# Order of the products, queries by token, and adjoining decay products in a hybrid decoder block on one core

## The chip, the core and the metric

The kernel runs on one core of a Trainium2 chip. What is measured is the device time of one execution in microseconds, the median of several runs. A NeuronCore has TensorE (matmuls, which write to PSUM), VectorE, ScalarE and GpSimd (elementwise work), and queues that issue DMA transfers; each engine works through its own instructions in order and waits for the others by semaphores. In the profile, PE is TensorE's matmuls, PEld its weight loads, DVE VectorE, ACT ScalarE, POOL GpSimd and SP the engine that issues most transfers.

## The reference

One decoder layer on 256 tokens with a model width of 2048, all in float32:

```python
h = rms_norm(x, norm_mix_w)
q, k, v, z, xbc, dt_raw, gate_a, gate_s = split(h @ w_in)      # 16960 columns
q = rms_norm(q per head, q_norm_w); k = rms_norm(k per head, k_norm_w)
attn = sliding_window_attention(q, k, v, attn_sinks, rel_bias_table) @ w_attn_out   # 32 heads of 64, 4 kv heads
ssm = mamba2_mixer(z, xbc, dt_raw, ...) @ w_ssm_out            # 64 heads of 64, 8 groups, chunks of 128
x = x + (sigmoid(gate_a) * attn + sigmoid(gate_s) * ssm) @ w_out
u = causal_depthwise_conv(rms_norm(x, norm_ffn_w) @ w_ffn_up)
g, up = split(u); x = x + (gelu(g) * up) @ w_ffn_down          # 5632 wide
x = x + sigmoid(rms_norm(x, ple_norm_w) @ w_ple_gate) * (p @ w_ple_proj)
```

In the mixer, `seg = exp(a_cum[l] - a_cum[s])` below the diagonal is the decay between two tokens of a chunk, and `y_diag = (cb * seg) @ xdt` is the product with it, per head and chunk. In the attention, a token sees the 128 tokens up to itself, with a bias by distance and one extra "sink" logit per head.

## The kernel before

Activations lie transposed, features on the 128 partitions and the 256 tokens along the row. Precision beyond one pass comes from splitting: a value is stored as a high part (rounded to the matmul's type) and a low part (the rest). An activation tile such as `XS[:, k, :]` holds the high parts of 256 tokens and then the low parts, 512 columns. The weights come from memory in chunks of 512 KB (four blocks of 128 rows, 256 output columns). `load_chunk` (L68) starts the transfer, lets ScalarE write the high part `wh` (L77) and VectorE the low part `wl` (L78); there are three buffers of each. `products` (L81) is one block of weights against one activation block: the high weights against all 512 columns (L84) and the low weights against the first 256 (L83, L86). The sum of the PSUM tile's two halves, which `summed` makes (L109), is the result.

A `panel` (L92) makes 256 output columns, that is two feature tiles of 128, each in a PSUM tile of its own (`acc`, four buffers). For every chunk it runs the four k of the first tile and then the four k of the second. `by_token` (L482) does the same with the roles exchanged, tokens on the partitions of the result: three matmuls of 256 columns for each k and half of the tokens (L494 to L496). Only keys and values use it.

The stages follow one another: the state-space mixer in 8 groups of five panels (two of `xc`, one of B and C, two of `z`); eight panels of its gate; `w_ssm_out`; keys and values; attention; `w_attn_out`; `w_out`; 44 panels of the feed-forward's first weight and the second weight; the gated embedding. The instructions are written in this order, but a planner orders those of each engine by a simulated timeline, in which the earlier written goes first when it is ready. So in the trace a panel's long products sometimes run one ahead of the short ones.

In a group of the mixer, GpSimd makes the decay exponents of one chunk (`E`, L359 and L360, 1024 columns, one buffer), ScalarE their exponential (L361), VectorE multiplies by `cbm` (L362), TensorE makes eight heads' products, alternately in the upper and the lower half of the output's partitions (L366), and VectorE adds the skip term (L370). Then the same comes for the second chunk, whose `E` needs the first one's buffer.

In the attention 16 panels alternate by `ATT_ORDER`: three of queries, then gate and query in turn, then three of gates. A query panel ends as two transposed tiles `qc`, one for each pair of heads. After every chunk of a panel `advance` gives each running `attend` one turn; at most three run at once, and a new one may start in each turn. An `attend` goes through five turns: (1) its bias is fetched, `head_rstd` gets the heads' norms from squares with four statistics matmuls (L472) and a power on GpSimd (L477), and the queries are split into `Q`, high part in the own half of the partitions and low part in the other; (2) scores with high and low keys (L557, L558), the latter with 64 rows, then scale and bias on VectorE; (3) softmax; (4) transposes (L590); (5) the output products (L597 to L599).

## Time and profile before

| | |
|---|---|
| median of 3 timed runs | 2117.54 us (2113.01 to 2117.91) |
| profiled execution, its own time | 2113.4 us |
| its span, first to last instruction | 2111.6 us |
| mean granted TensorE clock | 0.995 of full speed |
| busy: PE, PEld, DVE, ACT, POOL | 2094.0, 1815.8, 1511.2, 1176.4, 182.6 us |
| matmuls, VectorE and ScalarE instructions | 12228, 2526, 1775 |
| read from memory | 381 MB, 182 GB/s over the span |

Busy time of PE is time with at least one matmul in flight; the matmuls overlap, so what one costs is read from the starts of its neighbours. A wait of an engine that does not set the end costs nothing. In the rows below, "xN" merges N neighbouring instructions of one kind into one line, whose start is that of the first.

### The profile page before, as it was taken

Reading aid. Unit: us, or ns where it says so; the run is one execution under the profiler, and the core shown is the slowest. Engines: PE = TensorE matmul, PEld = TensorE weight load, DVE = VectorE, ACT = ScalarE, POOL = GpSimd, SP = SyncE. Lnnn points to the kernel's source line nnn. Section 1 sums busy time; section 2 is a strip of 40 time slices with the busy share of each in tenths; the row PEclk is TensorE's granted clock in tenths of the full one; section 3 lists DMA queues with packets and bytes.
Section 4 is the critical chain, followed back from the end, with each engine's and each line's share of the span. In section 5 each row is a group of like instructions: output and inputs, shape, how many; then the busy total and the mean of one; then the engine's idle time right before and its main releaser. Section 6 shows DMA issues by size and latency. Waiting matters only on the chain.

```text
span 2111.6 us, 32047 instructions
## 1 busy us (share of the span) xinstructions
PE 2094.0 (99%) x12228; PEld 1815.8 (86%) x12228; DVE 1511.2 (72%) x2526; ACT 1176.4 (56%) x1775; POOL 182.6 (9%) x122
## 2 busy tenths in 40 slices
PE   7999999999999999999999999999999999999999
PEld 6888888888888888888888888888888888888888
DVE  7888888888655456767667777777777776455576
ACT  5766766666544434656464556555555555444454
POOL 3212122211000000000000020000000000000000
PEclk8999999999999999999999999999999999999999
DMA  5565555555555555444335655555555555555564
GB/s 192 207 201 176 192 180 190 187 192 170 180 190 189 183 187 198 145 154 163 126 125 194 228 188 188 187 189 190 186 184 188 190 187 186 186 189 186 175 208 145
DMA packets 113302, 385.47 MB, mean 183 GB/s; under 512 B 14075, under 2 KB 21116, under 8 KB 111996
## 3 DMA queue, kind: packets, MB, share of 16 engines
q1 hardware_dynamic: 104060, 366.00, 50.5%
q10 hardware_dynamic: 9088, 17.43, 2.4%
q8 instruction: 95, 1.56, 0.3%
q14 instruction: 59, 0.48, 0.1%
HBM read 381.17 MB, written 2.21 MB: 182 GB/s over the span
## 4 chain that ended last, share of the span: by engine, by line
PE 96%; issue 1%; DVE 1%; DMA 1%; ACT 0%; POOL 0%; SPq 0%; ACTq 0%; POOLq 0%
PE acc L84 59%; PE acc L86 28%; PE acc L83 2%; PE ms L558 1%; PE ms L557 1%; PE ms L366 1%; PE ms L590 1%; PE acc L90 1%; DVE wl L78 0%; PE ms L597 0%; PE ms L84 0%; PE ms L472 0%; PE ms L346 0%; PE ms L377 0%; PE ms L599 0%
## 5 line engine op out<-in xcount | busy, mean ns | idle before, releaser
L78 DVE TENSOR_TENSOR wl<-raw,wh 128x1024 fp32r<-128x1024 f32 (+1 forms) x700 | 862.8, 1233 | 477.3 <-ACT wh L77 470.1
L77 ACT ACTIVATE wh<-raw 128x1024 fp32r<-128x1024 f32 (+1 forms) x700 | 733.0, 1048 | 655.4 <-PE acc L84 476.0
L84 PE MATMUL acc<-XS,wh 128*128 128x512 f32 x2048 | 717.4, 400 | 7.0 <-ACT wh L77 7.0
L84 PE MATMUL acc<-XG,wh 128*128 128x512 f32 x1632 | 559.2, 395 | 0.0
L86 PE MATMUL acc<-XS,wl 128*128 128x256 f32 x1920 | 533.9, 286 | 4.6 <-DVE wl L78 4.6
L84 PEld LDWEIGHTS acc<-XS,wh 128*128 128x128 f32 x2048 | 375.6, 191 | 77.8 <-ACT wh L77 7.2
L86 PE MATMUL acc<-XG,wl 128*128 128x256 f32 x1530 | 412.6, 281 | 0.0
L86 PEld LDWEIGHTS acc<-XS,wl 128*128 128x128 f32 x1920 | 365.2, 190 | 24.1 <-DVE wl L78 9.6
L84 PEld LDWEIGHTS acc<-XG,wh 128*128 128x128 f32 x1632 | 293.2, 188 | 54.0
L86 PEld LDWEIGHTS acc<-XG,wl 128*128 128x128 f32 x1530 | 287.1, 188 | 14.1
L84 PE MATMUL acc<-FS,wh 128*128 128x512 f32 x704 | 245.5, 397 | 0.0
L86 PE MATMUL acc<-FS,wl 128*128 128x256 f32 x688 | 189.5, 281 | 0.0
L84 PE MATMUL acc<-YS,wh 128*128 128x512 f32 x512 | 178.2, 395 | 0.0
L84 PEld LDWEIGHTS acc<-FS,wh 128*128 128x128 f32 x704 | 129.6, 188 | 28.5
L86 PE MATMUL acc<-YS,wl 128*128 128x256 f32 x496 | 137.0, 282 | 0.0
L86 PEld LDWEIGHTS acc<-FS,wl 128*128 128x128 f32 x688 | 129.2, 188 | 3.0
L112 ACT ACTIVATE lo<-acc 128x256 f32<-128x256 f32 x158 | 59.7, 383 | 93.9 <-PE acc L84 93.9
L84 PEld LDWEIGHTS acc<-YS,wh 128*128 128x128 f32 x512 | 94.1, 188 | 20.2
L662 POOL TENSOR_TENSOR sqa<-sqa,rsq 128x256 f32<-128x256 f32 x30 | 32.6, 1088 | 883.7 <-ACT rsq L661 882.8
L86 PEld LDWEIGHTS acc<-YS,wl 128*128 128x128 f32 x496 | 93.1, 188 | 2.2
L84 PE MATMUL acc<-AS,wh 128*128 128x512 f32 x256 | 88.5, 397 | 0.2 <-DVE sum L114 0.2
L84 PE MATMUL acc<-MS,wh 128*128 128x512 f32 x256 | 87.7, 396 | 0.0
(250 smaller groups left out, 2222.1 us busy)
## 6 DMA issues: line engine op xcount, KB each, us to landing
raw<-in_w_in SPq DMA_DIRECT2D x260, 512.0 KB, 3.3
raw<-in_w_ffn_up SPq DMA_DIRECT2D x176, 512.0 KB, 3.2
raw<-in_w_ffn_down SPq DMA_DIRECT2D x88, 512.0 KB, 3.2
raw<-in_w_ssm_out SPq DMA_DIRECT2D x64, 512.0 KB, 3.2
raw<-in_w_attn_out SPq DMA_DIRECT2D x32, 512.0 KB, 3.2
raw<-in_w_out SPq DMA_DIRECT2D x32, 512.0 KB, 3.3
raw<-in_w_ple_gate SPq DMA_DIRECT2D x32, 512.0 KB, 3.2
acb<-acd ACTq DMA_DIRECT2D x8, 1024.0 KB, 6.3
```

Of the source, the lines that this page charges most:

```text
L77: S.activation(wh[:, ks, :], raw[:, ks, :], AF.Copy)
L78: V.tensor_tensor(wl[:, ks, :], raw[:, ks, :], wh[:, ks, :].bitcast(F32), ALU.subtract)
L83: TE.matmul(ps[:, 0:T], lhsT=wl, rhs=x[:, 0:T], start=False, stop=False, skip_group_check=True)
L84: TE.matmul(ps, lhsT=wh, rhs=x, start=first, stop=last)
L86: TE.matmul(ps[:, 0:T], lhsT=wl, rhs=x[:, 0:T], start=False, stop=False, skip_group_check=True)
L90: TE.matmul(ps[:, 0:T], lhsT=w, rhs=x[:, h * T:(h + 1) * T], start=first and n == 0, stop=last and n == 2)
L112: S.activation(lo, ps[:, T:2 * T], AF.Copy)
L366: TE.matmul(py[r * HD:(r + 1) * HD, j * P:(j + 1) * P], lhsT=xdt[:, c, h * HD:(h + 1) * HD], rhs=E[:, h, :], start=True, stop=True)
L557: TE.matmul(ss[h][:, cs], lhsT=Q[:, h, qs], rhs=kh[g][:, ks], start=True, stop=False)
L558: TE.matmul(ss[h][:, cs], lhsT=Q[half[h], h, qs], rhs=kl[g][half[h], ks], start=False, stop=True)
L590: TE.transpose(pt[:, d * P:(d + 1) * P], Ls[:, h, c:c + P], ident)
L662: G.tensor_tensor(sqa, sqa, sq, ALU.add)
```

## The change

`products` takes both feature tiles of a block: high weights of tile one and two, then low weights of tile one and two. `panel` goes over k with both tiles in step, and so do the last panel (`products_joined`) and the embedding. In the mixer `decays` makes both chunks' exponentials at the start of a group, with two buffers of `E` (and one of `zg` in place of two); the product with the state, `po`, comes before the decay products, which follow one another for both chunks in two PSUM tiles. In attention the queries are made by token; `normed` takes the norms along the row (a square on ScalarE, a reduction on VectorE, the power on GpSimd) and scales the queries; `attend` has a first turn that only fetches the bias, then transposes its two heads' queries. The low keys' product takes all 128 rows. The order of the output products alternates between the two heads. `ATT_ORDER` puts the eight query panels into the first eleven.

```diff
@@ -37,8 +37,7 @@
-ATT_ORDER = ([("q", 0), ("q", 1), ("q", 2)] + [x for n in range(5) for x in (("g", n), ("q", n + 3))]
-             + [("g", 5), ("g", 6), ("g", 7)])
+ATT_ORDER = [(x[0], int(x[1])) for x in "q0 q1 q2 g0 q3 q4 g1 q5 q6 g2 q7 g3 g4 g5 g6 g7".split()]
@@ -78,16 +77,20 @@
-    def products(ps, wh, wl, x, first, last):
-        if last:
...
+    def products(ps2, wh, wl, x, first, last):
+        tiles = [slice(i * P, (i + 1) * P) for i in range(2)]
+        for ps, cs in zip(ps2, tiles):
+            TE.matmul(ps, lhsT=wh[:, cs], rhs=x, start=first, stop=False, skip_group_check=True)
+        for ps, cs in zip(ps2, tiles):
+            TE.matmul(ps[:, 0:T], lhsT=wl[:, cs], rhs=x[:, 0:T], start=False, stop=last, skip_group_check=True)
@@ -97,12 +100,10 @@
                 wh, wl = load_chunk(src[base + j])
-            for ct in range(2):
-                cs = slice(ct * P, (ct + 1) * P)
...
+            for k in range(KC):
+                kk = j * KC + k
+                (products_joined if joined else products)(ps, wh[:, k, :], wl[:, k, :], xs[:, kk, :],
+                                                          kk == 0, kk == nk - 1)
             if between:
@@ -213,6 +214,18 @@
         nc.sync.dma_start(gno, a["ssm_norm"])
+        def decays(acb, hs):
+            Es = []
+            for c in range(2):
+                E = sp.tile([P, 8, P], F32, name="E", bufs=2)
+                sa = bc(acs[:, c, hs].unsqueeze(2), [P, 8, P])
+                G.tensor_tensor(E, acb[:, :, c, :], sa, ALU.subtract)
+                G.tensor_tensor(E, E, bc(tri.unsqueeze(1), [P, 8, P]), ALU.mult)
+                S.activation(E, E, AF.Exp)
+                Es.append(E)
+            return Es
@@ -307,6 +320,7 @@
                 acb = sums_of_group(g)
+                Es = decays(acb, hs)
             xc = sp.tile([P, 4, T], F32, name="xc")
@@ -317,6 +331,7 @@
                     acb = sums_of_group(0)
+                    Es = decays(acb, hs)
                 for i in range(2):
@@ -351,30 +366,28 @@
-            yg = sp.tile([P, 4, T], F32, name="yg", bufs=1)
-            for c in range(2):
...
...
                 TE.matmul(po[:, js], lhsT=xde[:, js], rhs=cbm[:, 1, :], start=True, stop=True)
+            yg = sp.tile([P, 4, T], F32, name="yg", bufs=1)
+            for c in range(2):
+                E = Es[c]
+                V.tensor_tensor(E, E, bc(cbm[:, 2 * c, :].unsqueeze(1), [P, 8, P]), ALU.mult)
+            pys = [misc(), misc()]
+            for c in range(2):
+                for h in range(8):
+                    j, r = h // 2, h % 2
+                    TE.matmul(pys[c][r * HD:(r + 1) * HD, j * P:(j + 1) * P],
+                              lhsT=xdt[:, c, h * HD:(h + 1) * HD], rhs=Es[c][:, h, :], start=True, stop=True)
+            for c in range(2):
+                cs = slice(c * P, (c + 1) * P)
+                for j in range(4):
+                    V.scalar_tensor_tensor(yg[:, j, cs], xc[:, j, cs], dsk[:, 4 * g + j:4 * g + j + 1],
+                                           pys[c][:, j * P:(j + 1) * P], ALU.mult, ALU.add)
             ec = sp.tile([P, 512], F32, name="ec", bufs=1)
@@ -456,31 +469,31 @@
         V.tensor_scalar(nsink, sink, -1.0, None, ALU.mult)
         gq = ap.tile([P, 2], F32, name="gq", bufs=1)
...
-        def head_rstd(t, scale, nm):
-            sq = ap.tile([P, T], F32, name="hsq")
-            S.activation(sq, t, AF.Square)
-            st = misc()
+        def normed(ps2):
+            qm = ap.tile([P, 2, 4], F32, name="qm")
             for b in range(2):
-                TE.matmul(st[:, 2 * b:2 * b + 2], lhsT=sq[:, b * P:(b + 1) * P], rhs=blk64, start=True, stop=True)
-            v = ap.tile([P, 2, 2], F32, name="hv")
+                sq = ap.tile([P, 256], F32, name="ksq")
+                S.activation(sq, ps2[b][:, 0:PW], AF.Square, scale=HD ** -0.5)
+                V.tensor_reduce(qm[:, b, :], sq.rearrange("p (h d) -> p h d", h=4), AX.X, ALU.add)
+                V.tensor_scalar(qm[:, b, :], qm[:, b, :], r2_tok[:, b:b + 1], EPS, ALU.mult, ALU.add)
+            p = ap.tile([P, 2, 4], F32, name="qp")
+            G.tensor_tensor(p, qm, bc(mhalf[:, 0:1].unsqueeze(2), [P, 2, 4]), ALU.pow)
+            r = ap.tile([P, 2, 4], F32, name="qr")
+            qn = ap.tile([P, 2, PW], F32, name="qn", bufs=3)
             for b in range(2):
-                V.tensor_scalar(v[:, b, :], st[:, 2 * b:2 * b + 2], r2_tok[:, b:b + 1], EPS, ALU.mult, ALU.add)
-            p = ap.tile([P, 2, 2], F32, name="hp")
...
+                V.tensor_scalar(r[:, b, :], p[:, b, :], r_tok[:, b:b + 1], HD ** -0.5, ALU.mult, ALU.mult)
+                V.tensor_tensor(qn[:, b, :].rearrange("p (h d) -> p h d", h=4),
+                                ps2[b][:, 0:PW].rearrange("p (h d) -> p h d", h=4),
+                                bc(r[:, b, :].unsqueeze(2), [P, 4, HD]), ALU.mult)
+            return qn
+        def by_token(between=None):
@@ -494,6 +507,8 @@
                         TE.matmul(ps2[b][:, 0:PW], lhsT=lo, rhs=wh[:, k, :], start=False, stop=(kk == ND - 1))
+                if between:
+                    between()
             base += CH
@@ -538,30 +553,32 @@
-        def attend(i, qc):
+        def attend(i, qn):
...
             bias = pair_bias(i)
-            rq = head_rstd(qc, HD ** -0.5, "rq")
+            yield
+            qt = misc()
+            cs = slice((i % 2) * P, (i % 2 + 1) * P)
+            for b in range(2):
+                TE.transpose(qt[:, b * P:(b + 1) * P], qn[:, b, cs], ident)
             Ls = ap.tile([P, 2, 384], F32, name="Ls", bufs=3)
...
             for h in range(2):
-                S.activation(Q[half[h], h, :], qc[half[h], :], AF.Copy)
-                V.tensor_tensor(Q[half[1 - h], h, :], qc[half[h], :], Q[half[h], h, :].bitcast(F32), ALU.subtract)
+                S.activation(Q[half[h], h, :], qt[half[h], 0:T], AF.Copy)
+                V.tensor_tensor(Q[half[1 - h], h, :], qt[half[h], 0:T], Q[half[h], h, :].bitcast(F32), ALU.subtract)
             yield
             ss = [misc(), misc()]
-            for cs, ks, qs in ((slice(0, 256), slice(0, T), slice(P, T)), (slice(256, 384), slice(P, T), slice(0, P))):
-                for h in range(2):
+            for h in range(2):
+                for cs, ks, qs in ((slice(0, 256), slice(0, T), slice(P, T)),
+                                   (slice(256, 384), slice(P, T), slice(0, P))):
                     TE.matmul(ss[h][:, cs], lhsT=Q[:, h, qs], rhs=kh[g][:, ks], start=True, stop=False)
-                    TE.matmul(ss[h][:, cs], lhsT=Q[half[h], h, qs], rhs=kl[g][half[h], ks], start=False, stop=True)
+                    TE.matmul(ss[h][:, cs], lhsT=Q[:, h, qs], rhs=kl[g][:, ks], start=False, stop=True)
             for h in range(2):
-                s = ss[h]
-                V.scalar_tensor_tensor(Ls[:, h, 0:256], s[:, 0:256], rq[:, 1, h:h + 1], bias[:, h, :],
...
+                V.tensor_tensor(Ls[:, h, 0:256], ss[h][:, 0:256], bias[:, h, :], ALU.add)
+                V.tensor_tensor(Ls[:, h, 256:384], ss[h][:, 256:384], bias[:, h, 0:P], ALU.add)
             nm = ap.tile([P, 2, 2], F32, name="nm")
@@ -591,12 +608,12 @@
             o = misc()
-            for h in range(2):
-                rows = slice(h * HD, (h + 1) * HD)
...
+            vs = slice(g * HD, (g + 1) * HD)
+            for cs, b, ks, f, e in ((slice(0, P), 0, slice(0, P), True, True),
+                                    (slice(P, T), 0, slice(P, T), True, False),
+                                    (slice(P, T), 1, slice(T, 384), False, True)):
+                for h in range(2):
+                    TE.matmul(o[h * HD:(h + 1) * HD, cs], lhsT=vt[:, b, vs], rhs=pts[:, h, ks], start=f, stop=e)
             split(AS[:, i, :], o[:, 0:T])
@@ -610,14 +627,15 @@
         for kind, pn in ATT_ORDER:
+            if kind == "q":
+                qn = normed(by_token(advance))
+                waiting += [(2 * pn, qn), (2 * pn + 1, qn)]
+                continue
             ps2 = panel(W, base, ND, XS, between=advance)
...
             for i in range(2):
-                if kind == "q":
-                    waiting.append((2 * pn + i, summed(ps2[i], "qc", 5, ap)))
...
+                t = summed(ps2[i])
+                V.tensor_tensor(GA[:, 2 * pn + i, :], t, r_bc, ALU.mult)
         while waiting or running:
```

## Rows read from the trace of the kernel before

**Rows 1.** The chain that ended last, by line: share of the span.
```profile
PE acc L84 59%; PE acc L86 28%; PE acc L83 2%; PE ms L558 1%; PE ms L557 1%; PE ms L366 1%; PE ms L590 1%; PE acc L90 1%; DVE wl L78 0%; PE ms L597 0%; PE ms L84 0%; PE ms L472 0%; PE ms L346 0%; PE ms L377 0%; PE ms L599 0%
```

**Rows 2.** Busy time by stage: window, its length, PE, PEld, DVE, ACT, POOL, clock, DMA.
```profile
50.00:520.00 470.00, 469.66 (x2878) 408.84 (x2877) 408.10 (x672) 308.99 (x404) 104.23 (x53) 1.00 0.56 189
...
797.00:1105.00 308.00, 307.55 (x1869) 259.81 (x1867) 210.59 (x492) 175.94 (x372) 19.56 (x17) 0.99 0.45 151
...
1262.00:1757.00 495.00, 495.00 (x2824) 432.07 (x2823) 382.10 (x701) 291.65 (x442) 3.98 (x3) 1.00 0.54 188
```

**Rows 3.** Waits over the span: who for whom, us in total, times, longest.
```profile
ACT wh L77 <- PE acc L84: 476.0, 288, 5.9
...
PEld acc L86 <- DVE wl L78: 9.6, 11, 2.5
```

**Rows 4.** Timeline of PE, first panel of the ssm output: start us, us.
```profile
616.84 0.28 PE L86 MATMUL acc<-YS,wl 128*128 128x256 f32 x1
616.96 0.39 PE L84 MATMUL acc<-YS,wh 128*128 128x512 f32 x1
...
617.89 0.28 PE L86 MATMUL acc<-YS,wl 128*128 128x256 f32 x1
618.01 0.39 PE L84 MATMUL acc<-YS,wh 128*128 128x512 f32 x1
...
619.40 0.63 PE L84 MATMUL acc<-YS,wh 128*128 128x512 f32 x2
619.86 0.28 PE L86 MATMUL acc<-YS,wl 128*128 128x256 f32 x1
...
620.91 0.40 PE L86 MATMUL acc<-YS,wl 128*128 128x256 f32 x2
621.15 0.40 PE L84 MATMUL acc<-YS,wh 128*128 128x512 f32 x1
```

**Rows 5.** Timeline of PE in the values by token, 14 matmuls from first to last.
```profile
815.01 0.28 PE L494 MATMUL acc<-wh,XS 128*128 128x256 f32 x1
...
816.60 0.28 PE L496 MATMUL acc<-wh,XS 128*128 128x256 f32 x1
```

**Rows 6.** Timeline of PE in attention: output products, statistics, scores, next panel.
```profile
1078.06 0.43 PE L597 MATMUL ms<-pts,vt 128*64 128x128 f32 x2
...
1078.83 0.38 PE L599 MATMUL ms<-pts,vt 128*64 128x128 f32 x2
1079.14 0.61 PE L472 MATMUL ms<-blk,hsq 128*128 128x2 f32 x4
1079.61 0.36 PE L557 MATMUL ms<-kh,Q 128*128 128x256 f32 x1
...
1081.86 0.50 PE L84 MATMUL acc<-AS,wh 128*128 128x512 f32 x1
```

**Rows 7.** Timeline of PE in attention: six transposes and what follows.
```profile
1073.96 0.88 PE L590 MATMUL ms<-c_ident,Ls 128*128 128x128 f32 x6
1074.59 0.36 PE L86 MATMUL acc<-AS,wl 128*128 128x256 f32 x1
```

**Rows 8.** Timeline of PE in the mixer: second chunk's decay products and their neighbours.
```profile
96.38 0.40 PE L86 MATMUL acc<-XS,wl 128*128 128x256 f32 x2
96.71 1.09 PE L366 MATMUL ms<-E,xdt 128*64 128x128 f32 x16
97.73 0.94 PE L377 MATMUL ms<-cbm,xde 128*128 128x128 f32 x6
```

**Rows 9.** Timeline of POOL in the mixer: decay exponents.
```profile
158.95 2.74 POOL L360 TENSOR_TENSOR E<-E,tri 128x1024 f32<-128x1024 f32 x1
```

**Rows 10.** Timeline of DVE in the same stretch.
```profile
159.52 3.25 DVE L394 TENSOR_TENSOR yg<-yg,zg 128x1024 f32<-128x1024 f32 x1
```

**Rows 11.** That line's instructions: ns min/median/max, first and last start.
```profile
L394 DVE TENSOR_TENSOR yg<-yg,zg x8: 1211/3244/3320, 100.4 to 532.0; 128x1024 f32<-128x1024 f32 x8
```

**Rows 12.** Groups of instructions: count, busy us, mean ns, idle before.
```profile
L86 PEld LDWEIGHTS acc<-XS,wl 128*128 128x128 f32 x1920 | 365.2, 190 | 24.1 <-DVE wl L78 9.6
```

More of the change, by code (lines that the diff above doesn't have):

```diff
@@ L79, in load_chunk, with products_joined @@
         return wh, wl
-    def products(ps, wh, wl, x, first, last):
-        if last:
-            TE.matmul(ps[:, 0:T], lhsT=wl, rhs=x[:, 0:T], start=False, stop=False, skip_group_check=True)
-        TE.matmul(ps, lhsT=wh, rhs=x, start=first, stop=last)
-        if not last:
-            TE.matmul(ps[:, 0:T], lhsT=wl, rhs=x[:, 0:T], start=False, stop=False, skip_group_check=True)
-    def products_joined(ps, wh, wl, x, first, last):
-        for n, (w, h) in enumerate(((wh, 0), (wh, 1), (wl, 0))):
-            TE.matmul(ps[:, 0:T], lhsT=w, rhs=x[:, h * T:(h + 1) * T], start=first and n == 0, stop=last and n == 2)
+    def products(ps2, wh, wl, x, first, last):
[4 more added lines that the diff above has]
+            TE.matmul(ps[:, 0:T], lhsT=wl[:, cs], rhs=x[:, 0:T], start=False, stop=last, skip_group_check=True)
+    def products_joined(ps2, wh, wl, x, first, last):
+        for i, ps in enumerate(ps2):
+            cs = slice(i * P, (i + 1) * P)
+            for n, (w, h) in enumerate(((wh, 0), (wh, 1), (wl, 0))):
+                TE.matmul(ps[:, 0:T], lhsT=w[:, cs], rhs=x[:, h * T:(h + 1) * T], start=first and n == 0,
+                          stop=last and n == 2)
     def panel(src, base, nk, xs, before=None, between=None, joined=False):
@@ L99, in panel @@
                 wh, wl = load_chunk(src[base + j])
-            for ct in range(2):
-                cs = slice(ct * P, (ct + 1) * P)
-                for k in range(KC):
-                    (products_joined if joined else products)(
-                        ps[ct], wh[:, k, cs], wl[:, k, cs], xs[:, j * KC + k, :],
-                        j * KC + k == 0, j * KC + k == nk - 1)
+            for k in range(KC):
+                kk = j * KC + k
+                (products_joined if joined else products)(ps, wh[:, k, :], wl[:, k, :], xs[:, kk, :],
+                                                          kk == 0, kk == nk - 1)
             if between:
@@ L383, in hybrid_block @@
             V.tensor_tensor(yg[:, :, P:T], yg[:, :, P:T], ec.rearrange("p (j l) -> p j l", j=4), ALU.add)
-            zg = sp.tile([P, 4, T], F32, name="zg", bufs=2)
+            zg = sp.tile([P, 4, T], F32, name="zg", bufs=1)
             for pn in range(2):
@@ L708, in embedding @@
             wh, wl = load_chunk(a["w_ple_proj"][pn], 2, PW)
-            es = []
-            for i in range(2):
-                cs = slice(i * P, (i + 1) * P)
-                ps = misc()
-                for k in range(2):
-                    products(ps, wh[:, k, cs], wl[:, k, cs], PS_[:, k, :], k == 0, k == 1)
-                es.append(summed(ps, "ple", 4, pp))
-            return es
+            ps2 = [misc(), misc()]
+            for k in range(2):
+                products(ps2, wh[:, k, :], wl[:, k, :], PS_[:, k, :], k == 0, k == 1)
+            return [summed(ps, "ple", 4, pp) for ps in ps2]
         for pn in range(8):
```

34 lines of the change are left out of this document (removed).

## The prediction

> **What bounds the kernel now.** I read the chain of waits by line first, then the engines' busy time stage by stage, and only then single instructions. The chain that ended last runs through TensorE: 59% of the span through the long product of `products` (L84, the weight's high part against 512 columns) and 28% through the short one (L86, the low part against 256) [rows 1]. TensorE has work in flight without a break in the stages of [rows 2]. So a change counts by what it does to TensorE's starts, unless it makes an engine that feeds TensorE late. Three stages matter: the state-space stage (50 to 520 us), where VectorE is busy in 408 of 470 us; attention (797 to 1105 us), 211 of 308 us; and the plain panels, for which 1262 to 1757 us stands [rows 2]. Almost nothing is lost there to data that is late: TensorE's weight loads waited 9.6 us in all for a low part, whereas ScalarE waited 476 us for TensorE to give a buffer back [rows 3]. What a matmul costs is the time from its start to the next start, since the durations overlap; every price below is such a difference.
>
> The sum is made against the profiled execution's own 2113.4 us (span 2111.6 and 1.8 around it). The median of the three timed runs is 2117.5, their lowest 2113.0, so the profile lies at the fast end of them.
>
> **Part 1, the order inside `products`.** Before, a panel runs four k of one feature tile, long, short, long, short, and then four of the other. After, each k runs long, long, short, short, every one into the other PSUM tile than the one before it. It is 2592 such steps of four matmuls: 161 panels of 16 k (40 state-space, 8 gates, 16 for the ssm output, 8 gates in attention, 8 and 8 for the two output weights, 44 up, 22 down, 7 for the last gate) and 16 in the embedding. No matmul and no weight load is added or removed. All four kinds of step between neighbours stand in the trace of before, though rarely, because the planner already lets one run ahead. Long and short in turn: from 616.96 to 619.40 us seven pairs take 2.44 us, 0.349 each. Long after long: 0.46 us for two, 0.23 each, what a long one takes before a short one (0.349 less 0.12). Short after short: 0.24 for two, 0.12 each, as 616.84 to 616.96. And the change of tile at 618.01, where by the code the fifth pair begins in the other bank, comes 0.12 after its forerunner, like a step within one bank [rows 4]. So the four cost 0.70 us in either order, and I take 0 for this part. Its ends are wide because 2592 steps multiply anything: the by-token product of keys and values, which has the roles of weight and activation swapped, does 14 matmuls of 256 columns in 1.59 us, so 768 columns in 0.341 against 0.349 [rows 5]. If alternation reached that, it would be 5184 pairs by 0.009, 46 us less. At the other end, the timeline is resolved to 0.01 us; that much on two of the four steps is 52 us more.
>
> **Part 2, queries by token.** (a) A query panel becomes 96 matmuls of 256 columns, 96 by 0.1136 = 10.9 us [rows 5], for 32 pairs at 0.349 = 11.2 us: 0.26 us by 8 panels = 2.1 us less.
> (b) The score products, eight per pair of heads: the half-height ones against `kl` (64 rows) become full height. Before, the eight take from 1079.61 to 1081.86 us, 2.25 us [rows 6]; there are 16 pairs. Plain matmuls of 256 columns take 0.114 to 0.12, and those of 128 columns 0.105 by the transposes (six in 0.63 us) [rows 7]: four and four make 0.89 to 0.90. That is 1.35 by 16 = 21.6 us less, the largest term. If half of the present cost is not due to the height, 11 us; nothing excludes that, but ordinary matmuls of these widths stand in the same stage at the lower price.
> (c) The four statistics matmuls of a pair go (1079.14 to 1079.61, 0.47 us [rows 6]); two transposes come, 0.21 us by the same six [rows 7]: 0.26 by 16 = 4.2 us less.
> (d) The output products, twelve recorded matmuls in 1.08 us (1078.06 to 1079.14 [rows 6]), get the alternation of column halves that the decay products have, 16 in 1.02 us [rows 8], 0.064 each: 0.77, so 0.31 by 16 = 5.0 us less; 0 if the planner had already reached what alternation gives.
> (e) On the other engines a pair loses a square, four small VectorE operations, one GpSimd power and the sum into `qc`; a panel gains two squares, two reductions, four small operations, two products and one power. VectorE's work per pair stays about even, so I cost it at nothing: TensorE covers it, with 308 us to VectorE's 211 [rows 2]. In the new order q panels crowd into the first eleven, and an `attend` has six turns and an end where it had five and an end; three at a time give 12/7 = 1.7 pairs per panel, all through by the 13th panel. If the cover is thin there, the splits of the next weight chunk are late; I allow 3 us.
>
> **Part 3, the state-space stage.** The two chunks' decay products adjoin. Each stands now as a run of its own: the two short matmuls before it take 0.33 us to its start instead of 0.24 [rows 8], so an entry costs 0.09; the exit lies between 0 and 0.18, as the last two output products of a pair take 0.31 us to the next kind (1078.83 to 1079.14 [rows 6]) where two within a run take 0.13. One entry and exit less in each of 8 groups: 0.7 to 2.2, I take 1.5 us less. The 4 GpSimd operations of a group move to its start, past the conv of the first panels; the exponentials go with them, ahead of ScalarE's weight copies. No DMA is added on a queue, and the bias and sums transfers are issued in the same order. The cover is the group's three panels of 11.2 us before the decays are multiplied. GpSimd's time collides with VectorE though: at 158.95 GpSimd begins 2.74 us on the decays, and VectorE's product of `yg` and `zg`, started at 159.52, takes 3.25 us; the same line's shortest is 1.21 [rows 9 to 11]. I allow 4 us for where the moved ones fall. The two-tile burst on VectorE (two products of this shape, 1.2 us each) also lies in that allowance.
>
> The Trainium skill, SBUF — State Buffer, "Who interferes with whom", says that a VectorE instruction with two SBUF inputs and a GpSimd instruction that reads SBUF exclude each other for a whole instruction. The trace agrees with 3.25 against 1.21 us. That rule speaks against this change, as the weight split itself has two SBUF inputs; its result is the third rival.
>
> **The end.** Both tiles of the last panel now finish together, so their last vector operations queue: below 1 us, taken as 0.3.
>
> **Sum.** 2113.4 - 2.1 - 21.6 - 4.2 - 5.0 - 1.5 + 3 + 4 + 0.3 = 2086.3; as the timed median lies a little above the profile, I say 2088 us.
>
> **Rivals.**
> 1. Alternation speeds the stream. For: the by-token products show that 768 columns can pass in 0.341 us [rows 5]. Against: those stay in one bank, and the present change of bank saves nothing [rows 4]. 2088 - 46 = 2042 us.
> 2. VectorE becomes the bound while queries crowd. VectorE's 211 us in attention less 72 splits (18 panels of four) at the 1.21 us that this shape takes undisturbed [rows 11] leave 124, 7.7 per pair with all around it. At 1.7 pairs a panel that is 4.9 + 13.1 = 18.0 us, against TensorE's 10.9 + 1.7 by some 2.5 = 15.2. Over 9 panels 25 us late, in place of the 3 allowed: 2110 us. Against: the durations overlap by several hundredths each, which makes 18.0 too high, and whatever is late can run in the last five g panels.
> 3. GpSimd blocks the weight splits. The second chunk's two operations (at most 2.74 us each [rows 9]) now lie in one run with the first's; if each holds up a split for its whole length and none of it is absorbed, 5.5 by 8 = 44 us in place of 4: 2128 us, no gain left. Against: VectorE has 62 us idle in that stage [rows 2], and as many such operations ran before. Half of it is likelier, 2106.
> 4. Slower: two short matmuls in a row leave no long one under which the next weight load hides. A load shows 0.19 us, so the short one's 0.12 already leans on overlap [rows 12]. It decides from 25/2592 = 0.010 us a step; at 0.02 a step it is 52 us, 2140 us. Against: short after short at 0.12 in the trace, but only now and then, never twice a step.
> That the planner does not follow the written order is possible too; it then undoes part 1, which is 0, and changes nothing here.
>
> **How the numbers follow.** Forecast 0.58, rival 1 0.14, rival 2 0.10, rival 3 0.08, rival 4 0.10. The forecast's own range is 2072 to 2102. From 2040 to 2118 leaves out rival 4, and the ends of 1 and 3, together 0.2. A measurement of this kernel can tell 0.3% from no change, 6 us: faster is below 2111. Faster: the forecast, rival 1, and most of rivals 2 and 3 (0.11 of 0.18), 0.83; within 0.3%: the rest of these two but for 0.01, and 0.02 of rival 4, 0.08; slower: the other 0.09.
>
> **What would show it.** Right: in the plain stages the step of four stays at 0.70 us, and 1262 to 1757 us still needs 495; attention shrinks by some 30 us; the eight score products take 0.9 us; no new wait of the weight loads for L78's line. Wrong: steps of 0.68 or 0.72 in the plain panels (rivals 1 and 4); VectorE near full between the first and eleventh panel of attention with TensorE waiting for low parts (2); weight splits of 3 us beside GpSimd at a group's start (3).

## The result and the profile after

The changed kernel takes 2090.05 us (median of four runs, 2089.55 to 2093.43), the kernel before beside it 2115.28: a ratio of 0.9884, 95% interval 0.9865 to 0.9904. Forecast were 2088 us. The profiled execution after took 2089.55 us (span 2087.7), 23.85 less than the 2113.4 of before. The total is right; by stages it is not made of the terms of my sum.

Where a stage begins is the first matmul that reads its moving tile. In us, with the runs that are told below (0 to YS is the state-space groups and their gates, "rest" the gated embedding to the span's end). The stages are those of the profiled executions, whose times lie up to 3 us from the medians:

| kernel | 0 to YS | ssm output | K/V to MS | w_out | ffn up | ffn down | rest |
|---|---|---|---|---|---|---|---|
| before | 616.6 | 180.4 | 374.5 | 89.9 | 495.4 | 248.3 | 106.5 |
| after | 628.9 | 176.6 | 355.7 | 89.9 | 486.7 | 244.1 | 105.7 |
| e1_alternate | 628.6 | 176.6 | 373.3 | 90.0 | 486.7 | 244.1 | 105.7 |
| e2_decays | 617.2 | 180.4 | 375.7 | 89.9 | 495.4 | 248.3 | 106.6 |
| e4_old_decays | 629.4 | 176.6 | 355.5 | 89.9 | 486.7 | 244.1 | 105.7 |
| e5_late_decays | 628.7 | 176.6 | 355.8 | 90.0 | 486.7 | 244.1 | 105.7 |
| e6_ssm_old_order | 617.1 | 176.6 | 355.5 | 90.0 | 486.7 | 244.1 | 105.8 |
| e7_ssm_last_chunk | 616.3 | 176.6 | 357.2 | 90.0 | 486.7 | 244.1 | 105.8 |
| e8_orders | 628.2 | 176.6 | 358.6 | 88.3 | 489.1 | 244.1 | 105.7 |
| e9_old_places | 629.1 | 176.6 | 352.4 | 90.0 | 486.7 | 244.1 | 105.8 |
| e10_pairs_by_tile | 627.1 | 176.6 | 354.4 | 90.0 | 486.7 | 244.1 | 105.8 |
| e11_late_gates | 607.1 | 176.6 | 375.7 | 90.0 | 486.7 | 244.1 | 105.8 |
| e12_four_splits | 645.0 | 176.6 | 357.7 | 90.0 | 486.7 | 244.1 | 105.8 |
| e13_together | 617.4 | 176.6 | 355.1 | 88.4 | 486.7 | 242.9 | 105.7 |

So the plain panels give 17.5 us, which I had at nothing; the attention gives 18.7 of the 29.9 forecast; and the state-space stage takes 12.3 more, where I had 2.5.

The chain that ended last in the kernel after, to [rows 1]: TensorE's two plain products fall from 87% to 80%, and VectorE's weight splits appear in it with 3%. About 6% are the queries, whose products by token now have lines of their own (L507 to L509).

```profile
PE acc L84 53%; PE acc L86 27%; DVE wl L77 3%; PE acc L508 2%; PE acc L507 2%; PE acc L509 2%; PE ms L616 1%; PE ms L383 1%; PE acc L92 1%; ACT wh L76 0%; PE ms L607 0%; POOL zg L410 0%; POOL zg L409 0%; ACT L226 0%; PE ms L84 0%
```

Busy time by stretch of the kernel after (columns as in [rows 2]); the second is the attention, the last its end.

```profile
50.00:520.00 470.00, 456.23 (x2786) 396.13 (x2785) 413.33 (x652) 302.43 (x397) 109.26 (x53) 0.99 0.53 184
805.00:1113.00 308.00, 298.95 (x2196) 271.16 (x2195) 223.53 (x504) 178.16 (x372) 18.13 (x9) 0.99 0.49 163
1252.00:1738.00 486.00, 486.00 (x2822) 427.91 (x2821) 371.78 (x698) 281.66 (x443) 2.92 (x3) 1.00 0.55 191
...
1050.00:1100.00 50.00, 40.95 (x256) 34.07 (x256) 32.96 (x85) 30.34 (x72) 0.00 (x0) 0.93 0.31 105
```

In the state-space stage TensorE, which had work in flight in 469.7 of 470 us, now has none in 13.8. In the attention it has none in 9, all of them between 1050 and 1100 us, at a granted clock of 0.93, a mean between the levels of 2.4 and 1.2 GHz; in the kernel before this stretch had no gap:

```profile
1050.00:1100.00 50.00, 50.00 (x298) 41.57 (x297) 33.73 (x89) 31.40 (x69) 3.88 (x3) 1.00 0.40 137
```

The waits of the kernel after over the span, to [rows 3], first those for splits, then one that is new, the matmul for a group's norm waiting for GpSimd's sum of squares:

```profile
ACT wh L76 <- PE acc L84: 482.9, 299, 4.7
...
PEld acc L86 <- DVE wl L77: 20.7, 19, 2.9
PE acc L86 <- DVE wl L77: 12.0, 16, 2.5
...
PEld ms L413 <- POOL zg L410: 3.9, 6, 0.7
```

The step of four matmuls, over the whole of three stages of the kernel after (first and last start; 256, 128 and 352 steps of four):

```profile
L84 PE MATMUL acc<-YS,wh x512: 387/392/395, 628.9 to 805.1; 128*128 128x512 f32 x171
...
L84 PE MATMUL acc<-MS,wh x256: 389/396/399, 1161.3 to 1250.7; 128*128 128x512 f32 x128
...
L84 PE MATMUL acc<-FS,wh x704: 387/393/399, 1737.9 to 1981.5; 128*128 128x512 f32 x176
```

A stage's time by its steps is 0.690 us in the ssm output (176.6 by 256), 0.693 in ffn down (244.1 by 352) and 0.691 in ffn up (486.7 by 704); in w_out it is 0.702 (89.9 by 128), as before. The other three took 0.704 or 0.705 before.

The attention's small products in the kernel after, to [rows 6]:

```profile
899.19 0.43 PE L616 MATMUL ms<-pts,vt 128*64 128x128 f32 x2
899.56 0.39 PE L508 MATMUL acc<-wl,XS 128*128 128x256 f32 x1
...
900.11 0.87 PE L616 MATMUL ms<-pts,vt 128*64 128x128 f32 x10
900.91 0.38 PE L577 MATMUL ms<-kh,Q 128*128 128x256 f32 x1
...
906.93 0.28 PE L577 MATMUL ms<-kh,Q 128*128 128x256 f32 x1
907.05 0.28 PE L578 MATMUL ms<-kl,Q 128*128 128x256 f32 x1
907.16 0.22 PE L577 MATMUL ms<-kh,Q 128*128 128x128 f32 x1
907.22 0.28 PE L578 MATMUL ms<-kl,Q 128*128 128x128 f32 x1
907.33 0.33 PE L508 MATMUL acc<-wl,XS 128*128 128x256 f32 x1
907.50 0.28 PE L509 MATMUL acc<-wh,XS 128*128 128x256 f32 x1
...
908.92 0.28 PE L509 MATMUL acc<-wh,XS 128*128 128x256 f32 x1
...
1061.31 0.88 PE L616 MATMUL ms<-pts,vt 128*64 128x128 f32 x12
1062.11 0.38 PE L577 MATMUL ms<-kh,Q 128*128 128x256 f32 x1
```

One head's four score products take 0.40 us (906.93 to 907.33), a pair's eight 0.80. The twelve output products take 0.80 in one run (1061.31), but in 10 of 16 pairs two go ahead alone, 0.37 (899.19 to 899.56), and the ten behind them take the same 0.80 (900.11 to 900.91). The by-token products of the queries stand 0.118 apart (twelve in 1.42 us, 907.50 to 908.92), where those of keys and values stood 0.114 apart before [rows 5].

### The profile page after: what moved, and what is told of

Read it like the earlier page. It is cut to its first block, busy times and chain, and to the rows that moved or that the text cites. A ratio compares the mean times of both kernels' runs of the same rounds, so it can differ in the third digit from the quotient of the medians.

```text
span 2087.7 us, 32510 instructions
## 1 busy us (share of the span) xinstructions
PE 2046.4 (98%) x12452; PEld 1801.5 (86%) x12452; DVE 1502.7 (72%) x2510; ACT 1149.1 (55%) x1757; POOL 181.5 (9%) x114
## 3 DMA queue, kind: packets, MB, share of 16 engines
q8 instruction: 97, 1.59, 0.3%
## 4 chain that ended last, share of the span: by engine, by line
PE 91%; DVE 4%; issue 2%; ACT 1%; POOL 1%; DMA 1%; SPq 0%; DVEq 0%; ACTq 0%; POOLq 0%
PE acc L84 53%; PE acc L86 27%; DVE wl L77 3%; PE acc L508 2%; PE acc L507 2%; PE acc L509 2%; PE ms L616 1%; PE ms L383 1%; PE acc L92 1%; ACT wh L76 0%; PE ms L607 0%; POOL zg L410 0%; POOL zg L409 0%; ACT L226 0%; PE ms L84 0%
## 5 line engine op out<-in xcount | busy, mean ns | idle before, releaser
L76 ACT ACTIVATE wh<-raw 128x1024 fp32r<-128x1024 f32 (+1 forms) x700 | 733.4, 1050 | 806.5 <-PE acc L84 482.9
L84 PE MATMUL acc<-XS,wh 128*128 128x512 f32 x1792 | 570.8, 398 | 9.6 <-ACT wh L76 9.5
L84 PE MATMUL acc<-XG,wh 128*128 128x512 f32 x1632 | 506.6, 392 | 0.0
L86 PE MATMUL acc<-XS,wl 128*128 128x256 f32 x1792 | 363.3, 283 | 12.1 <-DVE wl L77 12.0
L86 PE MATMUL acc<-XG,wl 128*128 128x256 f32 x1632 | 322.7, 279 | 0.0
L84 PEld LDWEIGHTS acc<-XS,wh 128*128 128x128 f32 x1792 | 276.5, 190 | 13.6 <-ACT wh L76 11.0
L84 PEld LDWEIGHTS acc<-XG,wh 128*128 128x128 f32 x1632 | 247.2, 188 | 0.0
L86 PE MATMUL acc<-FS,wl 128*128 128x256 f32 x704 | 138.9, 279 | 0.0
L86 PE MATMUL acc<-YS,wl 128*128 128x256 f32 x512 | 101.0, 279 | 0.0
L508 PE MATMUL acc<-wl,XS 128*128 128x256 f32 x320 | 90.9, 284 | 0.0
L509 PE MATMUL acc<-wh,XS 128*128 128x256 f32 x320 | 90.1, 282 | 0.0
L507 PE MATMUL acc<-wh,XS 128*128 128x256 f32 x320 | 90.1, 282 | 0.0
```

The source lines that it names most:

```text
L76: S.activation(wh[:, ks, :], raw[:, ks, :], AF.Copy)
L84: TE.matmul(ps, lhsT=wh[:, cs], rhs=x, start=first, stop=False, skip_group_check=True)
L86: TE.matmul(ps[:, 0:T], lhsT=wl[:, cs], rhs=x[:, 0:T], start=False, stop=last, skip_group_check=True)
L507: TE.matmul(ps2[b][:, 0:PW], lhsT=hi, rhs=wh[:, k, :], start=(kk == 0), stop=False)
L508: TE.matmul(ps2[b][:, 0:PW], lhsT=hi, rhs=wl[:, k, :], start=False, stop=False)
L509: TE.matmul(ps2[b][:, 0:PW], lhsT=lo, rhs=wh[:, k, :], start=False, stop=(kk == ND - 1))
```

## The experiments

**One part at a time.** e1 puts only the new order of products into the kernel before, e2 only the state-space part; e4 takes the state-space part out of the changed kernel, and e5 leaves it in but puts the decays back to their place behind the transposes:

```diff
 # e1, to the kernel before
+        for ps, cs in zip(ps2, tiles):
+            TE.matmul(ps, lhsT=wh[:, cs], rhs=x, start=first, stop=False, skip_group_check=True)
+        for ps, cs in zip(ps2, tiles):
+            TE.matmul(ps[:, 0:T], lhsT=wl[:, cs], rhs=x[:, 0:T], start=False, stop=last, skip_group_check=True)
 # e2, to the kernel before (e4 takes the same out of the changed one)
+                Es = decays(acb, hs)
...
+            pys = [misc(), misc()]
 # e5, to the changed kernel
-                Es = decays(acb, hs)
...
+            Es = decays(acb, hs)
             po = misc()
```

> The kernel before with the alternating order alone (products, products_joined, panel, embedding); the decays and the attention as before. Theory A (the alternating order itself shortens every plain step of four matmuls, as the changed kernel's 486.7 us in ffn up against 495.4 and 176.6 in the ssm output against 180.4 suggest): ffn up 487, ffn down 244, ssm output 177, state-space and gate panels 1.75% below 616.6, so 606; in all about 28 us less, 2087. My forecast (order without effect): ffn up 495, in all 2115. Rival B (the order makes the state-space stage late, since both tiles' weights and both accumulators are wanted at once): ffn up 487 but the state-space stage near 629, in all 2105.

> The kernel before with the state-space part alone (decays at the group's start, both chunks' products adjoining, E in two buffers, zg in one); the order of products and the attention as before. Theory A (this part costs about 22 us in the state-space stage, hidden in the sum by the alternation): state-space stage 616.6 to about 637, in all 2136. Rival B (the alternation costs it): state-space stage 615 to 618, in all 2114. My forecast for this part: +2.5 us.

> The changed kernel with the state-space part as before; alternation and attention as changed. Theory A (state-space part costs about 22 us): state-space stage near 606, in all 2068. Rival B (the alternation costs it): near 629, in all 2090.

> The changed kernel with the call of decays put behind the transposes, just ahead of the products, where the kernel before had it; E stays in two buffers, zg in one, both chunks' products still adjoin. Theory A1 (the place costs it: GpSimd's two passes and the exponentials lie beside the group's first panels and hold back the splits of weights): state-space stage near 606, in all 2068. Rival A2 (what is bunched up costs it: both chunks' multiplications on VectorE one behind the other ahead of sixteen products, or zg in one buffer): state-space stage stays near 629, in all 2090. Rival A3 (the products now wait for the decays): above 640, in all over 2100.

Measured: e1 2107.05 us, ratio 0.9969 (0.9957 to 0.998); e2 2116.95, 1.0015 (1.0005 to 1.0024); e4 2090.12, 0.9896 (0.9879 to 0.9912); e5 2090.08, 0.9892 (0.9877 to 0.9907). Theory A of e2 and e4, which had the decays cost the state-space stage its time, fell: with them alone the stage is 617.2, without them 629.4, with them late 628.7 (e5's A2 had that number, but e4, in which nothing is bunched up, has it too). Rival B holds: the new order alone makes it 628.6. Alternation is worth 17.5 us in the plain panels and loses 12.0 of them here. What is late costs more than that: at the 0.012 us a step that ffn up gains (8.7 us by 704 steps), the stage's 48 panels of 16 steps should have gained some 9 us (an estimate).

The state-space part is not free, though. From 50 to 120 us TensorE has no work in flight for 5.2 us in e2, 5.0 in the kernel after and 4.6 in e5, where the kernel before has no gap and e1 and e4 have 2.1. In e2, which has none from 120 to 520 us, the later groups give it back. The waits in e1's groups from 120 to 600 us:

```profile
PEld ms L402 <- POOL zg L399: 10.7, 6, 1.8
PE ms L402 <- POOL zg L399: 8.1, 6, 1.4
PEld acc L85 <- ACT wh L77: 3.0, 13, 0.3
```

One of them, in e1's timeline of all engines:

```profile
172.31 1.04 ACT L397 ACTIVATE zg<-yg 128x1024 f32<-128x1024 f32 x1
...
173.43 1.29 POOL L398 TENSOR_TENSOR zg<-zg 128x512 f32<-128x512 f32 x1 [5.61 <-ACT zg L397]
...
174.33 1.47 DVE L78 TENSOR_TENSOR wl<-raw,wh 128x1024 fp32r<-128x1024 f32 x1 [1.75 <-ACT wh L77]
174.35 0.73 PE L85 MATMUL acc<-XS,wh 128*128 128x512 f32 x2
174.79 1.59 POOL L399 TENSOR_TENSOR zg<-zg 128x256 f32<-128x256 f32 x1
...
176.44 0.61 PE L402 MATMUL ms<-ones,zg 128*128 128x1 f32 x4 [1.36 <-POOL zg L399]
176.91 0.48 PE L87 MATMUL acc<-XS,wl 128*128 128x256 f32 x2
```

TensorE reaches the norm's matmul in its queue, and the squares' sum is not there yet; everything behind it stands for 1.4 us. The sum of 256 columns took GpSimd 1.59 us here beside VectorE's split; the shortest of that line takes 0.81. But GpSimd's length is not what decides: in e6 below that line's median is 1.60 too, and nobody waits from 120 us on. Behind four of the six waits, which are 1.4 us long each, the granted clock falls; the four stretches of 60 us from 240 to 480 us have 0.97, while the first and the last wait leave it at 1.00. In the kernel after, where no gap of TensorE from 120 to 520 us is longer than 0.53 us, it doesn't fall there. In e1:

```profile
120.00:180.00 60.00, 58.55 (x364) 50.85 (x363) 50.18 (x83) 38.33 (x51) 14.32 (x7) 1.00 0.54 179
...
300.00:360.00 60.00, 58.55 (x355) 50.70 (x354) 49.05 (x83) 36.19 (x48) 15.37 (x7) 0.97 0.57 190
```

**Is it the order in that stage?** e6 gives the eight groups' panels the old order and lets all behind them alternate; e7 gives only the last of a panel's four chunks the old order. e9 puts the query panels back to their old places.

```diff
 # e6 (e7: and j == nk // KC - 1)
+            if in_ssm[0]:
+                for i in range(2):
+                    cs = slice(i * P, (i + 1) * P)
+                    for k in range(KC):
+                        kk = j * KC + k
+                        product(ps[i], wh[:, k, cs], wl[:, k, cs], xs[:, kk, :], kk == 0, kk == nk - 1)
...
 # e9
-ATT_ORDER = [(x[0], int(x[1])) for x in "q0 q1 q2 g0 q3 q4 g1 q5 q6 g2 q7 g3 g4 g5 g6 g7".split()]
+ATT_ORDER = ([("q", 0), ("q", 1), ("q", 2)] + [x for n in range(5) for x in (("g", n), ("q", n + 3))]
+             + [("g", 5), ("g", 6), ("g", 7)])
```

> The changed kernel with the old order of products (tile by tile, long and short in turn) in the panels of the eight state-space groups alone; everything behind them alternates. Theory A (the alternation costs the 12 us in the state-space stage): stage 0 to YS about 616 to 618 against 628.9, no wait of over 0.5 us for GpSimd's zg or VectorE's wl from 120 us on, in all about 2078. Rival (the loss hangs on something else in the stage): 626 to 630, in all 2089.

> The changed kernel with the old order in the last of a panel's four chunks alone, and only in the state-space groups: tile 0's bank is then complete 1.4 us ahead of tile 1's, as in the kernel before, and three chunks of four still alternate. Theory A1 (both banks coming complete at once bunches their evacuation, and what follows it, sums on GpSimd and splits on VectorE, comes late): stage near 611, in all about 2072. Rival A2 (the written order of the queues comes out otherwise for any change of the products' order, and the waits are where it puts them): anywhere from 617 to 630, with waits at other lines; in all 2078 to 2091.

> The changed kernel with the query panels at their old places (up to the thirteenth panel instead of the eleventh), still by token. If finishing the queries early is worth something: K/V to MS longer than the changed kernel's 355.7 us, 358 to 362, in all 2092 to 2096. If the last pairs are late anyway, whatever the place (14 us of waits inside the attention's output product in the changed kernel): 354 to 357, in all 2088 to 2091. My forecast gave the places no time of their own.

Measured: e6 2080.57 us, 0.9845 (0.9829 to 0.9862); e7 2081.21, 0.9846 (0.9831 to 0.9861); e9 2087.45, 0.9877 (0.9863 to 0.9892). e6 confirms it: 617.1 us, and all that is left of TensorE's waits from 120 to 600 us is this:

```profile
PEld acc L93 <- issue: 1.2, 7, 0.2
```

From 50 to 120 us e6 still has 5.1 us without work, like the others with the state-space part. e7 is no better than the old order throughout (616.3 against A1's 611), though three chunks of four alternate; its weight loads wait 8.4 us for low parts. e9's K/V to MS is 3.3 us shorter, not longer; the whole is the same within the intervals. Finishing the queries early earns nothing.

**Why does the new order speed the plain panels, and why not in w_out?** e8 runs ffn up in six orders, seven panels each, and moves MS by a pad:

```diff
+            "a": [(p, i, k) for k in ks for p in "hl" for i in (0, 1)],
+            "b": [(p, i, k) for i in (0, 1) for k in ks for p in "hl"],
+            "c": [(p, i, k) for k in ks for i in (0, 1) for p in "hl"],
+            "d": [(p, i, k) for i in (0, 1) for m in (0, 2) for p in "hl" for k in (m, m + 1)],
+            "e": [x for k in ks for x in (("h", 0, k), ("h", 1, k), ("l", 1, k), ("l", 0, k))],
+            "f": [(p, i, k) for i in (0, 1) for p in "hl" for k in ks],
...
     MS = ms_pool2.tile([P, ND, 2 * T], F32R, name="MS")
+    ms_pad = ms_pool2.tile([P, 40], F32, name="ms_pad")
```

> The changed kernel with six orders of the sixteen products of a chunk in ffn up, seven panels each: a h0 h1 l0 l1 (as changed), b tile by tile h l h l (as before), c h0 l0 h1 l1, d tile by tile h h l l, e h0 h1 l1 l0, f tile by tile four h then four l (h long, l short, the number the tile). A panel takes 11.05 us in order a and 11.25 us in order b by the traces so far. H1 (long behind long and short behind short is what is faster): a, d, e, f 11.05, b and c 11.25. H2 (changing the accumulator's bank is what is faster): a, c 11.05, e in between, b, d, f 11.25. H3 (the fewer changes between long and short, the faster): f under 11.0. Beside it, in w_out alone, a 160-byte pad moves the moving tile MS (the stage that showed no gain, 89.9 us before and after): if its place decides, 88.3; if not, 89.9.

Measured (one run): a panel from its first matmul to the next one's takes 11.04 us in a, 11.16 in b, 11.23 in c, 11.04 in d, 11.04 in e, 11.07 in f (the usual value of the seven). H1 is right for the orders whose lengths ran as written, which are all but c: where equal lengths always follow one another a panel is faster, though by 0.12 us and not by 0.20. Longer runs of equals bring no more, so H3 fell (f). Changing the bank does nothing by itself: by the code d stays in one bank for eight matmuls and is as fast as a. Order b, then c, then d, in e8's timeline of TensorE:

```profile
1353.16 0.40 PE L94 MATMUL acc<-XG,wh 128*128 128x512 f32 x1
1353.39 0.28 PE L94 MATMUL acc<-XG,wl 128*128 128x256 f32 x1
...
1355.95 0.39 PE L94 MATMUL acc<-XG,wh 128*128 128x512 f32 x1
...
1425.03 0.62 PE L94 MATMUL acc<-XG,wh 128*128 128x512 f32 x2
1425.49 0.40 PE L94 MATMUL acc<-XG,wl 128*128 128x256 f32 x2
1425.72 0.40 PE L94 MATMUL acc<-XG,wh 128*128 128x512 f32 x1
...
1427.83 0.63 PE L94 MATMUL acc<-XG,wh 128*128 128x512 f32 x2
...
1519.92 0.62 PE L94 MATMUL acc<-XG,wh 128*128 128x512 f32 x2
1520.37 0.40 PE L94 MATMUL acc<-XG,wl 128*128 128x256 f32 x2
...
1524.75 0.62 PE L94 MATMUL acc<-XG,wh 128*128 128x512 f32 x2
```

In b eight pairs in 2.79 us are 0.698 for two; in d seven steps in 4.83 us are 0.690. The planner reordered c: as it ran, a panel has three places of h h l l among strict turns, and behind such a place the turns come slower, six in 2.11 us, 0.703 for two. The kernel before ran in that way too, not in b's strict turns. Each of its panels in ffn up has four places with two long products in a row and four with two short ones, such as these, and takes 11.24 us:

```profile
1354.91 0.63 PE L84 MATMUL acc<-XG,wh 128*128 128x512 f32 x2
...
1356.42 0.40 PE L86 MATMUL acc<-XG,wl 128*128 128x256 f32 x2
```

So an equal neighbour now and then doesn't help, it costs. Of the 0.20 us that a panel gains, 0.08 come from leaving the irregular order (11.24 to 11.16) and 0.12 from equal lengths in pairs (11.16 to 11.04).

And the place of the moving tile decides whether there is a gain: MS, moved by 160 bytes, needs 88.3 us for its stage, 0.690 a step, against 0.702.

```profile
L84 PE MATMUL acc<-MS,wh x256: 388/392/397, 1163.4 to 1251.3; 128*128 128x512 f32 x128
```

**Can the state-space stage keep the gain?** e10 takes order d everywhere; e12 gives the splits a buffer more. e11 tries the end of the attention: two panels that need only XS go behind its last panel.

```diff
 # e10: in a chunk, for each tile i, for m in (0, 2)
+                for k in (m, m + 1):
+                    TE.matmul(ps, lhsT=wh[:, k, cs], rhs=xs[:, k0 + k, :], ...)
+                for k in (m, m + 1):
+                    TE.matmul(ps[:, 0:T], lhsT=wl[:, k, cs], rhs=xs[:, k0 + k, 0:T], ...)
 # e12: raw bufs 5 -> 3, wh and wl bufs 3 -> 4
 # e11: behind the last attention panel
+        for pn in range(2):
+            ps2 = panel(W, base, ND, XS)
...
+                S.activation(t, t, AF.Sigmoid)
+                V.tensor_tensor(T1[:, 2 * pn + i, :], T1[:, 2 * pn + i, :], t, ALU.mult)
```

> The changed kernel with the products tile by tile, two long then two short (order d of the earlier run, as fast there as the alternating order, 11.04 us a panel), in all panels of feature tiles. It keeps the equal lengths behind one another and gives back the early end of tile 0's bank. If both findings hold: plain stages as in the changed kernel (ffn up 486.7, ffn down 244.1, ssm output 176.6), state-space stage 606 to 611 (628.9 changed, 616 to 617 with the old order there), in all 2067 to 2073. If the waits of the state-space stage come with any faster stream, since VectorE and GpSimd can't follow it: stage 615 to 629, in all 2076 to 2090.

> The changed kernel with four buffers each for the split weights (wh, wl) and three for the raw weights instead of three and five, the same room in all: the splits may run one chunk of weights, 2.8 us, further ahead of TensorE, the loads two chunks less. If TensorE waits in the state-space groups because VectorE's and ScalarE's splits come up to 0.7 us late in a crowded stretch, which a chunk more of lead covers: a group 60.5 to 61.5 us against 63.25, stage 610 to 618, in all 2072 to 2080. If the two engines are simply full there, or the written order puts the splits late whatever the buffers: 625 to 631, in all 2087 to 2092. If three raw buffers are too few for the loads (3.3 us from issue to landing): every stage longer, over 2100.

> The changed kernel with two of the eight panels of the state-space output's gate (22.1 us of work that needs only XS) moved from ahead of the ssm output to behind the last attention panel, ahead of w_attn_out; their two tiles each are multiplied there. If TensorE waits in w_attn_out only because no other work is left while the last pairs finish: state-space and gates 606.8, K/V to MS 355.7 + 22.1 less 8 to 13, so 365 to 370, in all 2077 to 2082. If the last pairs come as much later as there is more to do, for the written order paces them: K/V to MS 376 to 379, in all 2088 to 2091.

Measured: e10 2084.58 us, 0.9856 (0.984 to 0.9872); e12 2106.08, 0.9962 (0.9948 to 0.9976); e11 2087.94, 0.9874 (0.986 to 0.9889). In e10 the stage is 627.1: that both banks come complete together is not the cause, as a tile-wise order that is equally fast loses as much. It falls in the second branch of e10's expectation, by which the waits come with any faster stream. In e12 the waits for splits are gone from 120 us on, and the norm's matmul waits all the more; the stage takes 645.0 us. What the fourth buffers and what the two raw buffers less did there, this run can't tell apart; three raw buffers did not hurt the other stages. e12's waits from 120 to 600 us:

```profile
PEld ms L413 <- POOL zg L410: 15.8, 6, 2.6
PE ms L413 <- POOL zg L410: 13.9, 6, 2.3
```

e11's first theory fell too: of the 22 us moved, K/V to MS grew by 20.0 (375.7). Counted from the start of keys and values, the last output product begins at 302.9 us (783.8 to 1086.7) instead of 284.6 (805.5 to 1090.1), so the last pairs come later with the work that was put ahead of them.

**All that helped.** e13 is e6 with the query panels at their old places, MS moved, and FS moved by 128 bytes in the same way.

```diff
+        fs_pad = fp.tile([P, 32], F32, name="fs_pad", bufs=1)
         FS = fp.tile([P, NF, 2 * T], F32R, name="FS", bufs=1)
```

> The earlier kernel with the old order of products in the state-space groups (2080.6 us; alternating behind them), with three things more: the 160-byte pad that moves MS in w_out (89.9 to 88.35 us in its run), a 128-byte pad that moves FS in ffn down likewise, and the query panels at their old places, still by token (K/V to MS 352.4 against 355.7 us). If they add up: stage 0 to YS 617, w_out 88.3, K/V to MS 352 to 353, and ffn down 243.0 instead of 244.06 if FS's place costs it the little by which it stands behind ffn up (0.2 us in 50); in all 2074 to 2076. If the place of FS has no part in that: ffn down 244.06, in all 2075 to 2077. If the gain of the old places hangs on what lies ahead of them: K/V to MS 355 to 356, in all 2077 to 2079.

Measured: 2073.56 us, ratio 0.9812 (0.9798 to 0.9825), the fastest of all. w_out 88.4 and ffn down 242.9 as expected, 0.690 a step in the latter (242.9 by 352):

```profile
L85 PE MATMUL acc<-FS,wh x704: 388/392/394, 1724.2 to 1966.6; 128*128 128x512 f32 x176
```

The old places' 3.3 us are not seen again (355.1); K/V to MS lies anywhere from 354 to 359 in kernels that share the changed attention (e4 to e8, e10 and e12).

## Why the prediction was right, and where it was not

The total was right, 2088 against 2090.05, and that it came out to 2 us is luck: the terms were wrong in both directions. The plain panels gave 17.5 us that I had at nothing; the state-space stage took 9.8 more than I had allowed, and the attention gave 11.2 less.

- *Part 1, "I take 0 for this part"* is the step that failed. I priced the step of four from neighbours that stood in the trace of before now and then: long after long 0.23, short after short 0.12 [rows 4]. In a regular run the four take 0.690 (11.04 us a panel), and the kernel before took 0.703 (11.24), more than the 0.697 of the seven turns that I read. The difference of 0.013 is about the resolution of those rows, and I had named that as the end of the range, not weighed it. Rival 1 was the mechanism with the wrong reason and size: not the other bank (e8, order d), and 17.5 us instead of 46. Its 46 was also a slip: 0.349 less 0.341 is 0.008, not 0.009, which makes 41.
- The same part had a second half that I did not see: I costed the order by TensorE's starts alone. In the state-space stage it costs 12 us by waits (e1, e6). My allowance of 4 us stood under Part 3, for the decays.
- *Part 3* was right in size: -1.5 and +4 forecast, +0.6 in its stage in e2, and 1.0015 for the whole, 3.6 us. The allowance of 4 for where the moved ones fall has its like in the first group (5.2 us without work in e2, from 50 to 120 us), but not for their place, since e5 has 4.6. Rival 3 is out: with the decays moved back or the part undone the time is the same (e5, e4). GpSimd and VectorE do hold each other up, 1.59 us for 0.81 (e1), but that costs TensorE nothing where nobody waits for it (e6). The Trainium skill, SBUF — State Buffer, "Who interferes with whom", on which rival 3 drew, agrees with the 1.59.
- *(b) scores* was the best term: 2.25 to 0.80 us where a pair's eight run together. Six of the sixteen pairs had two runs of 1.03 to 1.12 before, and some runs after have a slower entry (900.91: 0.50 for one head's four), which makes about 21.5 in all for 21.6. How much of it the full height gives is not shown: the order by heads changed with it, and no run has one without the other. *(c)*: the statistics' 0.47 (0.36 in seven pairs) went, two transposes cost mostly 0.14 to 0.17; about 4.3 for 4.2. *(d) outputs*: 0.80 when they run together, but split into two and ten in 10 pairs, which makes (10 by 1.17 + 6 by 0.80) / 16 = 1.03 against 1.08: 0.8 us for 5.0. *(a)*: the 2.1 did not come. 96 products at 0.118 are 11.3 us, not 10.9, and with what interrupts them the 10 by-token panels take 11.56 us each, no less than others.
- *(e)* failed in its place: "all through by the 13th panel" did not happen. The last pair's output products come at 1089.5 us, 40 us after w_attn_out has begun, whose panels need them. The gaps there are 9 us, and at 0.93 of the clock 50 us lose about 3.5 more; together that is 12.5, about what the attention's 18.7 lack of 21.5 + 4.3 + 0.8 and the 3.2 of its 16 plain panels (0.2 each, 11.24 to 11.04; e1, which changes nothing else there, got 1.2). These terms are read from the trace; no run has one of them alone. I had allowed 3, for splits in the crowded phase; rival 2 put the loss there too, and there it was not.

What stays open: why a regular run of equal pairs is the fastest, and why the end of a group comes late under the faster orders. Shown are the cause (the order of products in that stage) and the places of the waits (the norm's matmul, or a split); shown is that neither the decays nor banks complete together are the reason, and that a fourth split buffer in place of two raw ones is no cure. Which engine's order makes the difference was not found; nor what paces the last pairs, which earlier queries (e9) and other work (e11) did not change, nor why the by-token products stand 0.118 apart instead of 0.114.

## What to carry to other kernels

A regular order can be priced only from a regular run: irregular neighbours hide a hundredth of a microsecond, and thousands of steps multiply it. The order of before needs the same care: look in the trace at what ran, not at what is written, and divide a whole stage by its steps. Price a faster stream also by what feeds it: a stage in which VectorE is busy in 87% of the time gave nothing, and took 12 us. And read a result by stages: here they were off by 17.5, 9.8 and 11.2 us under a total that was right to 2.

## What the runs showed of the hardware

- Two matmuls of 512 columns and two of 256 take 0.690 us from start to start where they come in pairs of equals throughout, 0.698 where they take turns strictly (e8, orders a and b), and 0.703 to 0.705 where an equal neighbour breaks the turns now and then (e8, order c; the kernel before in three stages). The PSUM bank makes no difference (e8, order d).
- That gain hangs on where the moving tile lies in SBUF. MS had none of it and, moved by 160 bytes, has all (0.702 to 0.690 a step; e8, and again e13); FS had most of it and, moved by 128 bytes, has all (0.693 to 0.690; e13). By the tile sizes in the code, YS and XG, which had the gain from the start, begin at the same place within 256 bytes as each other, and FS began 128 bytes off it. The addresses themselves stand in no trace. Other places, and the old order with MS moved, were not tried.
